# Layer 1's expert passes finished in their own turn, gathered outputs added earlier, and the late tiles' modulation written with dealt columns in its last step

## The chip, the cores and the metric

The kernel runs on one core of a Trainium2 chip. The metric is the device time of one execution in microseconds. A core has a matrix engine (PE, with its weight loads shown as PEld), a vector engine (DVE), a scalar engine (ACT), GpSimd (POOL), and SP, which here does little but issue transfers. "Q" behind an engine's name (SPq, ACTq) means its instruction queue: registers, branches, transfers. The core's transfers share 16 DMA engines.

## The reference, cut to what matters

Two layers of a transformer over 256 latent and 256 context rows of 1024 columns. Each layer ends in a mixture of experts:

```python
def modulate(x, shift, scale):
    return layer_norm(x) * (1 + scale) + shift

xl = layer_norm(ALPHA * xl + g1 * yl, ln1_g[l], ln1_b[l])       # after the output projection
yl = moe(modulate(xl, sh2, sc2), router_w, ...)                 # 16 experts, two of one group per row
xl = layer_norm(ALPHA * xl + g2 * yl, ln2_g[l], ln2_b[l])
```

An expert computes `(silu(h @ gate) * (h @ up)) @ down` with 256 hidden columns, so its weights are 1 MB each for gate, up and down. Layer 0 handles latent and context rows (four tiles of 128 rows), layer 1 only the latent rows (two tiles). The output is the latent rows after layer 1.

## The kernel before

**The rows before the experts.** `out_proj` (L1201) computes for each tile of 128 rows the residual and the first layer norm, then the rows that the experts read: `rows_modulate` (L1348, one DVE operation, (x - mean) * sc2) and, after the router has been worked out, `rows_shift` (L1353, one DVE operation, times r plus sh2). Both go over 128x1024 f32. The result, the tile hx, has its columns dealt: column p*8+t of x stands at t*128+p, because a later transpose takes blocks of 128 columns and the weights of an expert are loaded with p outside t. Before the change, modulate does the dealing: it reads x and sc2 at a step of 8 elements (`dealt`, L1344) and writes contiguously; shift reads hx contiguously and sh2 at a step of 8 elements, and writes hx in place. hx then goes to a table H in DRAM, from which POOL gathers the rows of a pass (xb), and for the first pass PE picks rows straight from hx (`block_pick`, xbp<-oh,hx).

In both layers the last two tiles' modulations sit at the end of `out_proj`: modulate of the tile before the last (p), then of the last one (end), the router's small DVE operations on "arena", then both shifts back to back, then the tables of the routing (ids of the experts in "metai", a flag "anyi" that rows overflowed, "oh" and "roh" for picking rows).

**The passes.** `moe` (L1911) works in passes of 128 rows; a pass covers one expert or several. Layer 0 has 11 passes, layer 1 has eight, over the units (0,1), (2,3), (4,7), (5,6), (8,11), (9,10), (12,15), (13,14); `end` is 7 there. A unit's expert is known only on the chip. The weights of units 0 to 3 (W0) are loaded before, at the end of `out_proj`. A pass is: rows transposed (xT), `gate_up` (32 matmuls of 512 columns for a pass of four segments, 16 for two; PE, pgu), `act` (ACT th, DVE ac twice, PE transposes acp, ACT acT), `down` (PE, y), and `rows_out` (copies yo, then one 0.5 MB write to the table Y, issued by ACT).

`fetch(p + 2)` in each turn (L1915) issues the weights of the pass two ahead from SP. `expert_steps` (L1772) splits one unit's load in three steps: half 0 of gate and up (2 x 0.5 MB, into a raw buffer, four of these), half 1 (2 x 0.5 MB, into a u buffer, eleven of these), and down (1 MB, u; every fifth load puts half 0 in u and down into two h buffers as two transfers of 0.5 MB). Two units of one pass were interleaved step by step:

```python
for fs in zip(*steps):
    for f in fs:
        f()
```

SP works its queue in order: a transfer whose buffer is not free holds all that stand behind it. A few hundred instructions for rows that overflow their pass stand behind a branch in each layer (`overflow`, L1848); it isn't taken in the profiled execution, but each engine passes through it at its place.

**The order of a turn.** The loop (L1957) does `gate_up(p)`, `rows_of(p + 1)`, `fetch(p + 2)`, and `finish(*prev)` (L1967), which is act, down and Y write of pass p-1. A scheduler then places these by priority, so that y(p-1) lands in the matmul stream inside gate_up(p+1). After the loop come the broadcast loads, the gathers of Y's rows (`y_gather`, L1900, per tile two indirect transfers from POOL of 0.5 MB each: yg), and the last two passes (L2073): down of pass end-1, kept on the core as ylast, gate_up of the last pass, its act and down. What ylast holds is added by matmuls (pcomb, in `part`); what was gathered is scaled and added to x by `scale` (L2015: ACT yg, then DVE yg) and `add` (L2020: DVE yg, DVE x). In layer 1 (`mod is None`) they stand around the ylast copies, tile 0's ahead of them and tile 1's behind. `join` (DVE rest, x), then norm and output end the kernel. In layer 0 the tail also loads and splits the next layer's first weights (`split`: wraw, whi, wlo).

Of the kernel before, what the change touches and what calls it, by code (L numbers as in the profile page):

```python
# [15 lines left out]
OP = mybir.AluOpType  # L16
# [4 lines left out]
P = 128  # L21
D = 1024
KT = D // P
# [129 lines left out]
class Net:  # L153
# [1190 lines left out]
    def dealt(x):  # L1344

        return x.rearrange("r (p t) -> r t p", t=KT)

    def rows_modulate(self, k):  # L1348
        self.hx.append(k.h)
        k.hd = k.h[:, :D].rearrange("r (t p) -> r t p", t=KT)  # L1350
        self.nc.vector.scalar_tensor_tensor(k.hd, self.dealt(k.x), k.mean, self.dealt(self.sc2[:, k.s, :]), op0=OP.subtract, op1=OP.mult)

    def rows_shift(self, k, eng=None):  # L1353
        self.nc.vector.scalar_tensor_tensor(k.hd, k.hd, k.r[1], self.dealt(self.sh2[:, k.s, :]), op0=OP.mult, op1=OP.add)
        (eng or self.nc.sync).dma_start(self.H[self.l][k.n * P:(k.n + 1) * P, :], k.h[:, :D])

    def rows_turn(self, k, between=None):
# [550 lines left out]
    def moe(self, l, xs, tiles, mod):  # L1908
        nc, T = self.nc, len(tiles)
        streams = (0, 1) if T == 4 else (0,)  # L1910
        plan = unit_passes(l)  # L1911
        end = len(plan) - 1
        W = self.W0

        def fetch(p):  # L1915
            steps = []
            for _, _, a in plan[p][1] if p <= end else []:
                if a not in W:
                    W[a], new = self.expert_steps(l, self.meta(a, 15, engines=[mybir.EngineType.SP]))
                    steps.append(new)  # L1920
            for fs in zip(*steps):
                for f in fs:
                    f()

# [2 lines left out]
        def gather(p):  # L1927
            if p <= end:
                xb[p] = self.route_index(plan[p][0])

        def rows_of(p):
            xT = self.h([P, KT, P], "xT")
            if p == 0:
                self.block_pick(self.first, xT, lambda: gather(1))
            else:
                self.block_turn(xb[p], xT)
            return xT

        def finish(p, ps):
            ys = [self.pw("y2"), self.pw("y3")] if (end - p) % 2 else [self.po("y0"), self.po("y1")]  # L1940
            self.down(plan[p][1], W, self.act(ps), ys)
            self.rows_out(ys, plan[p][0] * P, self.p([P, D], "yo"))

        blocks, prev, got = {0: rows_of(0)}, None, []
        if T == 4:
            self.overflow(l)
        fetch(0)
        fetch(1)
        for p, (_, segs) in enumerate(plan[:-1]):
            gather(p + 2)  # L1950
            if p == 0 and l < DEPTH - 1:
                self.announce(l + 1, "SP", self.last_idx)
            ps = self.gate_up(segs, W, blocks[p], self.pa("pgu"))
            if p == 0:
                self.early_mm = self.last_mm
                if T == 2:
                    self.overflow(l)  # L1957
                else:
                    with self.behind(self.last_idx, self.last_mm):
                        self.ada_end()  # L1960
                for n in range(0, T, 2):
                    self.route_gates(n)
                self.route_rest()
            blocks[p + 1] = rows_of(p + 1)
            fetch(p + 2)
            if prev:
                finish(*prev)  # L1967
            prev = p, ps
            if p == end - 2:
                self.pickT = self.h([P, T, 2, P], "pickT")  # L1970
                for n in range(T):
                    self.last_rows(n)
# [22 lines left out]
        def split():  # L1995
            if self.late:
                self.late.pop(0)()

        def part(n, a):
            g = bag[n]  # L2000
            if a == 0:
                g.ps = [al("pcomb") for al in (self.pa, self.pw)]
            for c in range(2):
                nc.tensor.matmul(g.ps[c], self.pickT[:, n, spot[a]], yl[:, a, c], start=a == 0, stop=a == 1 and mod is None)
# [10 lines left out]
        def scale(n):  # L2015

            nc.scalar.activation(got[n][0], got[n][0], AF.Copy, scale=self.gab[:, 0, n:n + 1])
            stt(got[n][0], got[n][1], self.gab[:, 1, n:n + 1], got[n][0], op0=OP.mult, op1=OP.add)  # L2018

        def add(n):  # L2020
            x, y, i = xs[tiles[n]], got[n][0], 0 if tiles[n] in LAT_TILES else 1
            nc.vector.tensor_mul(y, y, g2[:, i, :])  # L2022
            stt(x, x, ALPHA, y, op0=OP.mult, op1=OP.add)  # L2023
# [46 lines left out]
        if mod is None:  # L2070
            steps = (mul, -1), (join, 0), (shift, 1), (centre, 0), (root, 0)
        else:
            steps = ((unit, 2), (join, 0), (shift, 1), (turn, 2), (more, 0), (centre, 0), (root, 1), (root, 0), (low, 2), (mul, -1))  # L2073
        with self.ordered(last):
            self.down(plan[end - 1][1], W, self.act(psA), ysA)
            for c in range(2):
                nc.scalar.copy(yl[:, 0, c], ysA[c])
            acB = self.act_rows(self.gate_up(plan[end][1], W, blocks[end], self.pa("pgu")))
            part(0, 0)
            aT = self.act_turn(acB)  # L2080
            split()
            self.down(plan[end][1], W, aT, ysB)
            part(1, 0)
            if mod is None:
                scale(0)
                add(0)
            nc.vector.tensor_copy(yl[:, 1, 0], ysB[0])
            nc.scalar.copy(yl[:, 1, 1], ysB[1])
            if mod is None:
                scale(1)  # L2090
                add(1)
            split()
            for t in range(-1, T + 2):
                for f, k in steps:
                    if 0 <= t - k < T:
                        f(t - k, tiles[t - k])
# [130 lines left out]
```

## Time and profile before

| | |
|---|---|
| three runs | 992.14, 987.21, 992.06 us; median 992.06 us |
| the profiled execution | 991.99 us, of which 990.2 us lie between its first and last instruction |
| busy share of the span | PE 86%, DVE 56%, ACT 34%, POOL 18% |
| DMA, mean | 232 GB/s over the span; 230.04 MB |
| mean granted clock of TensorE | 0.948 of full speed |

The busy shares are means over stages with different limits, so they don't tell what a stage waits for. The stages here: attention and output projection of layer 0 up to about 400 us, its experts to about 570, the same for layer 1 up to about 830 and 990. In the rows further on, a time is us from the span's start, "x3" counts instructions, and in square brackets stands how long the engine was idle before, and what ended that. A DMA share of 1.0 means that all 16 DMA engines were busy.

### The profile page before, as it was taken

The page shows a single profiled execution, that of the slowest core. Times are in us where ns is not written, and L with a number is a line of the kernel's source. Part 1 is how long each engine was busy: PE and PEld are TensorE (multiplying, and loading weights), DVE is VectorE, ACT ScalarE, POOL GpSimd, SP SyncE. Part 2 cuts the span into 40 slices and gives each one's busy share as a digit, 9 for nine tenths or more (in the row PEclk, how much of TensorE's full clock was granted, in tenths as well). Part 3 has the DMA queues.
Part 4 walks back from the last instruction along what each step waited for, and adds up shares of the span by engine and source line. Part 5 has one row for each costly group of instructions (what it writes and reads, how often), then busy time and mean ns, then how long its engine had stood idle before and what let it go on. Part 6 is the DMA issues. An engine that isn't in the chain of part 4 may idle for free. (4 is left out here: it accounts for less than half of the span.)

```text
span 990.2 us, 12986 instructions
## 1 busy us (share of the span) xinstructions
PE 848.4 (86%) x4436; PEld 465.8 (47%) x4436; DVE 549.7 (56%) x1419; ACT 332.7 (34%) x783; POOL 175.1 (18%) x195
## 2 busy tenths in 40 slices
PE   4799999999898982999999798999978964997773
PEld 2476555545345860643333245756654653332221
DVE  4465777567666679622221287677777577221116
ACT  2243455534454220011112248455474420110111
POOL 1522110002250111100010225132253010000010
PEclk9989999999999995999999899999999995999987
DMA  9963756465553248899999862155422493999981
GB/s 329 316 225 96 255 161 229 141 221 192 216 170 110 88 155 313 313 376 333 379 399 387 320 191 93 55 194 152 159 92 100 143 348 122 362 398 411 391 316 42
DMA packets 82150, 230.04 MB, mean 232 GB/s; under 512 B 10144, under 2 KB 26112, under 8 KB 77984
## 3 DMA queue, kind: packets, MB, share of 16 engines
q1 hardware_dynamic: 66624, 184.74, 52.5%
q10 hardware_dynamic: 11280, 29.21, 8.1%
q0 software_dynamic: 4176, 15.21, 4.0%
q8 instruction: 37, 0.61, 0.2%
q14 instruction: 33, 0.27, 0.1%
HBM read 215.97 MB, written 16.84 MB: 235 GB/s over the span
## 5 line engine op out<-in xcount | busy, mean ns | idle before, releaser
L1802 PE MATMUL pgu<-egu,xT 128*32 128x512 f32 (+2 forms) x752 | 152.7, 606 | 10.3 <-DMA egu<-in_exp_w_up_dram 9.9
L1040 ACT ACTIVATE P<-S,nm 128x512 f32<-128x512 f32 (+1 forms) x120 | 73.3, 614 | 77.8 <-DVE nm L1029 56.4
L262 PE MATMUL pw<-whi,xhi 128*128 128x512 f32 (+1 forms) x224 | 94.1, 422 | 4.5 <-ACT xhi L474 3.6
L264 PE MATMUL pw<-whi,xlo 128*128 128x512 f32 (+1 forms) x224 | 90.2, 406 | 4.1 <-DVE xlo L525 3.4
L1814 DVE SCALAR_TENSOR_TENSOR ac<-th,pgu 128x256 f32<-128x256 f32 x19 | 8.0, 421 | 154.3 <-ACT th L1812 154.3
L1802 PEld LDWEIGHTS pgu<-egu,xT 128*32 128x32 f32 (+2 forms) x752 | 47.2, 128 | 95.2 <-issue 92.4
L263 PE MATMUL pw<-wlo,xhi 128*128 128x512 f32 (+1 forms) x224 | 90.7, 406 | 0.0
L1832 PE MATMUL y<-edn,acT 128*32 128x512 f32 (+2 forms) x376 | 77.5, 625 | 6.1 <-DMA edn<-in_exp_w_down_dram 5.0
L1029 DVE TENSOR_REDUCE nm<-S 128x1 f32<-128x512 f32 (+1 forms) x120 | 68.4, 595 | 15.5 <-PE S L1002 11.0
L262 PEld LDWEIGHTS pw<-whi,xhi 128*128 128x128 f32 x224 | 43.1, 193 | 31.8 <-issue 16.2
L363 PE MATMUL adaacc<-adaw,cst 128*32 128x512 f32 x256 | 54.1, 606 | 0.0
L1703 POOL DMA_INDIRECT xb<-H,ridx x17 | 16.4, 963 | 196.1 <-DVE ridx L1700 66.6
L1070 PE MATMUL PTp<-ident,P 128*128 128x128 f32 x320 | 46.6, 277 | 3.7 <-DVE P L1058 3.4
L252 POOL TENSOR_TENSOR wolo<-woraw,wohi 128x512 fp32r<-128x512 f32 x32 | 41.0, 1309 | 48.7 <-ACT wohi L251 48.7
L264 PEld LDWEIGHTS pw<-whi,xlo 128*128 128x128 f32 x224 | 43.0, 192 | 14.0 <-DVE xlo L525 4.7
L1812 ACT ACTIVATE th<-pgu 128x256 f32<-128x256 f32 x19 | 7.3, 385 | 122.1 <-PE pgu L1802 109.0
L1832 PEld LDWEIGHTS y<-edn,acT 128*32 128x32 f32 (+2 forms) x376 | 23.2, 130 | 53.1 <-issue 38.4
L1070 PEld LDWEIGHTS PTp<-ident,P 128*128 128x128 f32 x320 | 35.9, 140 | 25.0 <-issue 15.3
L263 PEld LDWEIGHTS pw<-wlo,xhi 128*128 128x128 f32 x224 | 43.0, 192 | 10.0 <-issue 1.3
L262 PE MATMUL pwo<-wohi,oT 128*128 128x512 f32 x96 | 38.9, 406 | 0.7 <-ACT oT L256 0.7
L1077 ACT COPY PT<-PTp 128x512 f32<-128x512 f32 (+1 forms) x60 | 30.9, 515 | 21.9 <-PE PTp L1070 18.4
L264 PE MATMUL pwo<-wohi,oT 128*128 128x512 f32 x96 | 38.0, 395 | 0.0
(407 smaller groups left out, 1551.9 us busy)
## 6 DMA issues: line engine op xcount, KB each, us to landing
adaw<-in_w_ada_dram SPq DMA_DIRECT2D x32, 1024.0 KB
egu<-in_exp_w_gate_dram SPq DMA_DIRECT2D x64, 512.0 KB
egu<-in_exp_w_up_dram SPq DMA_DIRECT2D x64, 512.0 KB
edn<-in_exp_w_down_dram SPq DMA_DIRECT2D x26, 1024.0 KB
adaw<-in_w_ada_dram SPq DMA_DIRECT2D x32, 512.0 KB
wraw<-in_w_in_dram SPq DMA_DIRECT2D x20, 512.0 KB
woraw<-in_w_out_dram SPq DMA_DIRECT2D x8, 1024.0 KB
Y<-yo ACTq DMA_DIRECT2D x15, 512.0 KB
```

The costliest lines, as they stand in the source:

```text
L252: eng.tensor_sub(lo[:, s], src[:, s], hi[:, s].bitcast(F32))
L262: mm(out, a[0], b[0], start=start, stop=False)
L263: mm(out, a[0], b[1], start=False, stop=False)
L264: return mm(out, a[1], b[0], start=False, stop=stop)
L363: self.nc.tensor.matmul(acc[32 * j:32 * j + 32, :], self.cst[:, k if row is None else row, :], t[:, j, :], start=(k == 0), stop=stop)
L1029: nc.vector.tensor_reduce(t.nm[:, j:j + 1], t.S[j][:, :t.nk], axis=AX.X, op=OP.max, negate=True)
L1040: self.last_exp = nc.scalar.activation(t.P[:, j, :t.nk], t.S[j][:, :t.nk], AF.Exp, bias=t.nm[:, j:j + 1], accum_out=t.l[:, j:j + 1])
L1070: nc.tensor.transpose(t.pt[n][:, k, :], t.P[:, n, k * P:(k + 1) * P], self.ident)
L1077: (nc.vector.tensor_copy if t.kind != "A" and n == 0 else nc.scalar.copy)(out, t.pt[n][:, 0:nkt, :])
L1703: self.last_fetch = nc.gpsimd.indirect_dma_start(out=xb, out_offset=None, in_=self.H[self.l][:, :], in_offset=bass.IndirectOffsetOnAxis(ap ...
L1802: self.last_mm = mm(ps[c:c + w, :].rearrange("r (c n) -> r c n", c=2), xT[:, kk, c:c + w], W[a][kk // 4][:, :, kk % 4, :], start=kk == 0, ...
L1832: mm(ys[n][c:c + w, :], aT[:, f, c:c + w], W[a][2][f][:, n * 512:(n + 1) * 512], start=f == 0, stop=f == 1)
```

## The change

It has four parts. In `fetch`, two units of a pass are loaded one after the other (half 0, half 1, down of the first, then of the second), in both layers; only the last pass keeps the interleaving. In layer 1, a pass up to end-2 is finished in its own turn of the loop, `finish(p, ps)`, not in the next one's. In layer 1's tail, scale and add of both tiles stand ahead of the last pass's act. For the late tiles (tiles 2 and 3 of layer 0, both of layer 1) modulate reads and writes contiguously, and shift reads contiguously and writes with dealt columns into another buffer "hd": neighbouring elements of its output lie 128 elements (512 bytes) apart.

```diff
--- before.py
+++ after.py
@@ -1345,13 +1345,27 @@
 
         return x.rearrange("r (p t) -> r t p", t=KT)
 
+    @staticmethod
+    def dealt_out(x):
+        return x[:, :D].rearrange("r (t p) -> r p t", t=KT)
+
     def rows_modulate(self, k):
+        k.late = k.n >= self.T - 2
+        out, x, sc = k.h[:, :D], k.x, self.sc2[:, k.s, :]
+        if not k.late:
+            out, x, sc = out.rearrange("r (t p) -> r t p", t=KT), self.dealt(x), self.dealt(sc)
+        self.nc.vector.scalar_tensor_tensor(out, x, k.mean, sc, op0=OP.subtract, op1=OP.mult)
+
+    def rows_shift(self, k, eng=None):
+        src, sh = k.h[:, :D], self.sh2[:, k.s, :]
+        if k.late:
+            k.h = self.h([P, D], "hd")
+            out, src, sh = self.dealt_out(k.h), src.rearrange("r (p t) -> r p t", t=KT), sh.rearrange("r (p t) -> r p t", t=KT)
+        else:
+            out = src = src.rearrange("r (t p) -> r t p", t=KT)
+            sh = self.dealt(sh)
+        self.nc.vector.scalar_tensor_tensor(out, src, k.r[1], sh, op0=OP.mult, op1=OP.add)
         self.hx.append(k.h)
-        k.hd = k.h[:, :D].rearrange("r (t p) -> r t p", t=KT)
-        self.nc.vector.scalar_tensor_tensor(k.hd, self.dealt(k.x), k.mean, self.dealt(self.sc2[:, k.s, :]), op0=OP.subtract, op1=OP.mult)
-
-    def rows_shift(self, k, eng=None):
-        self.nc.vector.scalar_tensor_tensor(k.hd, k.hd, k.r[1], self.dealt(self.sh2[:, k.s, :]), op0=OP.mult, op1=OP.add)
         (eng or self.nc.sync).dma_start(self.H[self.l][k.n * P:(k.n + 1) * P, :], k.h[:, :D])
 
     def rows_turn(self, k, between=None):
@@ -1918,7 +1932,7 @@
                 if a not in W:
                     W[a], new = self.expert_steps(l, self.meta(a, 15, engines=[mybir.EngineType.SP]))
                     steps.append(new)
-            for fs in zip(*steps):
+            for fs in zip(*steps) if p == end else steps:
                 for f in fs:
                     f()
 
@@ -1963,7 +1977,9 @@
                 self.route_rest()
             blocks[p + 1] = rows_of(p + 1)
             fetch(p + 2)
-            if prev:
+            if T == 2 and p < end - 1:
+                finish(p, ps)
+            elif prev and T == 4:
                 finish(*prev)
             prev = p, ps
             if p == end - 2:
@@ -2075,20 +2091,17 @@
             self.down(plan[end - 1][1], W, self.act(psA), ysA)
             for c in range(2):
                 nc.scalar.copy(yl[:, 0, c], ysA[c])
+            for n in range(T) if mod is None else ():
+                scale(n)
+                add(n)
             acB = self.act_rows(self.gate_up(plan[end][1], W, blocks[end], self.pa("pgu")))
             part(0, 0)
             aT = self.act_turn(acB)
             split()
             self.down(plan[end][1], W, aT, ysB)
             part(1, 0)
-            if mod is None:
-                scale(0)
-                add(0)
             nc.vector.tensor_copy(yl[:, 1, 0], ysB[0])
             nc.scalar.copy(yl[:, 1, 1], ysB[1])
-            if mod is None:
-                scale(1)
-                add(1)
             split()
             for t in range(-1, T + 2):
                 for f, k in steps:
```

SP, the weights of pass 2 in layer 1 (units 4 and 7; the first loads its down weights as two transfers). A register instruction ahead of each transfer is left out. Before:

```order
L1885 TENSOR_LOAD metai_7656
...
L1763 DMA egu_8525<-in_exp_w_gate_dram 128x1024
...
L1763 DMA egu_8525<-in_exp_w_up_dram 128x1024
L1885 TENSOR_LOAD metai_7656
...
L1763 DMA egu_8528<-in_exp_w_gate_dram 128x1024
...
L1763 DMA egu_8531<-in_exp_w_gate_dram 128x1024
...
L1763 DMA egu_8534<-in_exp_w_gate_dram 128x1024
...
L1763 DMA edn_8537<-in_exp_w_down_dram 128x1024
...
L1763 DMA edn_8541<-in_exp_w_down_dram 128x2x1024
```

And now:

```order
L1899 TENSOR_LOAD metai_7658
...
L1777 DMA egu_8529<-in_exp_w_gate_dram 128x1024
...
L1777 DMA egu_8529<-in_exp_w_up_dram 128x1024
...
L1777 DMA egu_8532<-in_exp_w_gate_dram 128x1024
...
L1777 DMA edn_8535<-in_exp_w_down_dram 128x1024
L1899 TENSOR_LOAD metai_7658
...
L1777 DMA egu_8539<-in_exp_w_gate_dram 128x1024
...
L1777 DMA egu_8542<-in_exp_w_gate_dram 128x1024
...
L1777 DMA edn_8545<-in_exp_w_down_dram 128x2x1024
```

Unit 4's second half and its down weights now stand ahead of unit 7's first half.

PE in layer 1, from pass 4's rows to the last pass, before (y_9023 is the down projection of pass 4, y_9118 of pass 5, y_9156 of pass 6):

```order
L1802 MATMUL pgu<-egu,xT 32x512
L1832 MATMUL y_9023<-edn,acT 32x512 x8
L1832 MATMUL y_9024<-edn,acT 32x512 x8
L1897 MATMUL lastp<-ident,lastoh 128x128 x2
L1802 MATMUL pgu<-egu,xT 32x512 x31
L1737 MATMUL xbp<-ident,xb 128x128 x8
L1822 MATMUL acp<-ident,ac 128x128 x4
L1832 MATMUL y_9118<-edn,acT 64x512 x4
L1832 MATMUL y_9119<-edn,acT 64x512 x4
L1832 MATMUL y_9156<-edn,acT 32x512 x8
```

And now (y_9059 is pass 5, y_9160 pass 6):

```order
L1816 MATMUL pgu<-egu,xT 32x512
L1836 MATMUL acp<-ident,ac 128x128 x2
L1911 MATMUL lastp<-ident,lastoh 128x128 x2
L1816 MATMUL pgu<-egu,xT 32x512 x2
L1846 MATMUL y_9059<-edn,acT 64x512 x4
L1846 MATMUL y_9060<-edn,acT 64x512 x4
L1911 MATMUL lastp<-ident,lastoh 128x128 x2
L1816 MATMUL pgu<-egu,xT 32x512 x29
L1751 MATMUL xbp<-ident,xb 128x128 x8
L1836 MATMUL acp<-ident,ac 128x128 x2
L1846 MATMUL y_9160<-edn,acT 32x512 x8
```

Inside gate_up(6) stood the down projection of pass 4; now it is that of pass 5, and so in each turn of layer 1.

DVE in layer 1's tail, before:

```order
L1814 SCALAR_TENSOR_TENSOR ac_9207<-th_9205,pgu_9188 128x256
L1815 SCALAR_TENSOR_TENSOR ac_9207<-ac_9207,pgu_9188 128x256
L2018 SCALAR_TENSOR_TENSOR yg_9147<-yg_9148,arena_7648,yg_9147 128x1024
L2022 TENSOR_TENSOR yg_9147<-yg_9147,bc_9142 128x1024
L2023 SCALAR_TENSOR_TENSOR x_7635<-x_7635,yg_9147 128x1024
L2087 COPY ylast_9155<-y0_9158 128x512
L2018 SCALAR_TENSOR_TENSOR yg_9151<-yg_9152,arena_7648,yg_9151 128x1024
L2022 TENSOR_TENSOR yg_9151<-yg_9151,bc_9142 128x1024
L2023 SCALAR_TENSOR_TENSOR x_7637<-x_7637,yg_9151 128x1024
```

And now:

```order
L2034 SCALAR_TENSOR_TENSOR yg_9151<-yg_9152,arena_7650,yg_9151 128x1024
L2038 TENSOR_TENSOR yg_9151<-yg_9151,bc_9146 128x1024
L2039 SCALAR_TENSOR_TENSOR x_7637<-x_7637,yg_9151 128x1024
L2034 SCALAR_TENSOR_TENSOR yg_9155<-yg_9156,arena_7650,yg_9155 128x1024
L2038 TENSOR_TENSOR yg_9155<-yg_9155,bc_9146 128x1024
L2039 SCALAR_TENSOR_TENSOR x_7639<-x_7639,yg_9155 128x1024
L1828 SCALAR_TENSOR_TENSOR ac_9219<-th_9217,pgu_9200 128x256
L1829 SCALAR_TENSOR_TENSOR ac_9219<-ac_9219,pgu_9200 128x256
L2103 COPY ylast_9159<-y0_9162 128x512
```

The six operations on yg and x stood behind the last pass's ac, three of them behind the ylast copy; now all six stand ahead of ac. ACT's two yg likewise stand ahead of the last pass's th, where they stood behind its acT.

## Rows read from the trace of the kernel before

**Rows 1.** Windows: us, PE PEld DVE ACT POOL busy (count), PEclk, DMA share, GB/s.

```profile
835.00:839.50 4.50, 4.37 (x24) 2.89 (x24) 1.51 (x13) 0.59 (x1) 0.66 (x1) 0.80 0.50 161
839.50:845.00 5.50, 5.48 (x25) 2.22 (x26) 2.74 (x14) 0.00 (x0) 0.28 (x1) 1.00 0.64 208
...
867.00:892.00 25.00, 23.14 (x156) 9.08 (x149) 6.84 (x20) 3.86 (x8) 1.88 (x2) 1.00 1.01 398
...
917.00:942.00 25.00, 19.50 (x135) 6.62 (x133) 4.20 (x8) 3.76 (x9) 0.00 (x0) 0.93 1.02 391
```

**Rows 2.** Timeline of SP in layer 1: start us, us, transfer issued.

```profile
831.64 0.34 SPq L1763 DMA_DIRECT2D egu<-in_exp_w_up_dram  x1
841.49 0.33 SPq L1763 DMA_DIRECT2D egu<-in_exp_w_gate_dram  x1
```

**Rows 3.** Waits of SP's queue, 780 to 990 us: us in all, times, longest.

```profile
SPq L1763 <- PE pgu L1802: 9.8, 2, 8.9
```

**Rows 4.** Timeline of PE, pass 0's gate_up in layer 1, behind the overflow branch.

```profile
839.52 6.19 PE L1802 MATMUL pgu<-egu,xT 128*64 128x512 f32 x26
```

**Rows 5.** The chain that ended last, its end: start us, us, what.

```profile
941.72 20.12 DMA edn<-in_exp_w_down_dram
...
961.88 5.93 PE y L1832 x14
...
968.43 1.06 ACT yg L2017
...
969.51 1.29 DVE yg L2018
...
970.83 1.23 DVE yg L2022
...
972.08 1.22 DVE x L2023
973.31 0.61 DVE rest L2032
```

**Rows 6.** Timeline of DVE at the end of layer 0's output projection.

```profile
370.32 2.09 DVE L1351 SCALAR_TENSOR_TENSOR hx<-x,lnm,bc 128x1024 f32<-128x1024 f32 x1
...
379.50 2.04 DVE L1351 SCALAR_TENSOR_TENSOR hx<-x,bmv,bc 128x1024 f32<-128x1024 f32 x1
```

**Rows 7.** Windows, layer 0; columns as in rows 1.

```profile
446.00:448.00 2.00, 2.00 (x24) 0.63 (x20) 0.00 (x0) 0.00 (x0) 0.00 (x0) 1.00 0.18 47
...
480.00:520.00 40.00, 38.11 (x198) 14.51 (x196) 10.00 (x29) 5.42 (x11) 5.29 (x5) 1.00 1.02 401
...
380.00:384.00 4.00, 0.00 (x0) 0.00 (x0) 3.38 (x13) 0.21 (x1) 1.96 (x1) 0.50 0.36 102
```

**Rows 8.** Timeline of ACT, layer 0's tail: the next layer's weights awaited.

```profile
565.45 1.90 ACT L555 CAST whi<-wraw 128x2048 fp32r<-128x2048 f32 x1 [5.01 <-DMA wraw<-in_w_in_dram]
```

**Rows 9.** Timeline of DVE at the end of layer 1's output projection.

```profile
808.44 1.28 DVE L1339 SCALAR_TENSOR_TENSOR hx<-x,bmv,bc 128x1024 f32<-128x1024 f32 x1
...
813.12 2.04 DVE L1351 SCALAR_TENSOR_TENSOR hx<-x,bmv,shsc 128x1024 f32<-128x1024 f32 x1
...
821.11 2.05 DVE L1354 SCALAR_TENSOR_TENSOR hx<-hx,lnr,shsc 128x1024 f32<-128x1024 f32 x1
```

**Rows 10.** Timeline of PE: layer 1's pcomb.

```profile
953.14 1.98 PE L2004 MATMUL pcomb<-ylast,pickT 128*128 128x512 f32 x4
...
967.73 5.42 PE L2004 MATMUL pcomb<-ylast,pickT 128*128 128x512 f32 x12
```

**Rows 11.** Timelines of ACT, POOL, DVE: last Y writes, first gather, first use.

```profile
929.14 0.33 ACTq L1837 DMA_DIRECT2D Y<-yo  x1
...
943.19 0.33 ACTq L1837 DMA_DIRECT2D Y<-yo  x1
...
952.00 0.94 POOL L1903 DMA_INDIRECT yg<-Y,yslot  x1 [47.51 <-DMA bc<-in_ln_g_dram]
...
962.58 1.28 DVE L2018 SCALAR_TENSOR_TENSOR yg<-yg,arena 128x1024 f32<-128x1024 f32 x1 [8.04 <-DMA yg<-Y,yslot]
```

## The prediction, made before the changed kernel was run

> **What bounds the kernel now.** I read the chain of waits first, backwards from the end, then windows with the DMA share along it, then the timelines of SP, DVE and PE at the places where that share falls.
>
> The chain ends so: a transfer of down weights of the last pass, issued at 941.72, lands 20.12 us later at 961.84; the last down projection takes 5.93 us; then ACT yg, three DVE operations on yg and x (1.06, 1.29, 1.23, 1.22 us), and at 973.31 the first rest, which opens the norm [rows 5]. So two things set the end of layer 1: when the stream of weights is through, and what stands between the last y and rest.
>
> The stream itself: from 867 to 892 and from 917 to 942 the DMA engines are full (share 1.01 and 1.02, 391 to 398 GB/s), with PE busy 23.14 and 19.50 of 25 us [rows 1]. There nothing helps but fewer bytes or an earlier start. The start is not full: from 835 to 839.5 the share is 0.50, to 845 it is 0.64 [rows 1]. That is 4.5*0.50 + 5.5*0.36 = 2.25 + 1.98 = 4.23 us of 16 idle engines. The reason stands in SP's timeline: after unit 4's first half (issued up to 831.64) the next transfer goes out at 841.49 [rows 2], and SP's longest wait for a gate-up matmul is 8.9 us [rows 3]. Unit 7's first half wants a raw buffer that pass 0 still reads, and all else stands behind it.
>
> Layer 0 looks alike on a smaller scale: its experts run with DMA share 1.02 from 480 to 520, PE busy 38.11 of 40 us, but 446 to 448 has 0.18 [rows 7], and at the end ACT waits 5.01 us for the next layer's weights until 565.45 [rows 8]. Those are the last transfers of the same stream.
>
> **The change part by part.** The sum is made against the profiled execution, 991.99 us; the median of the runs is 992.06, so the two may stand for each other.
>
> 1. *Modulate of late tiles, layer 0.* Two operations of 2.09 and 2.04 us read two operands at a step of 8 elements [rows 6]. With both contiguous they become what the same shape costs elsewhere with contiguous operands, 1.28 [rows 9]: 0.81 + 0.76 = 1.57 us. DVE is the path here: the second unit's weights are issued right behind the last modulate, and from 380 to 384 the DMA engines idle for 4*0.64 = 2.56 us [rows 7]. An earlier issue moves the saturated stream behind it, and with that the weights at 565.45. Taken in full: -1.57.
>
> 2. *Modulate, layer 1.* The last one, 2.04 us at 813.12 [rows 9], has the router behind it without a gap: -0.76. The one before it is followed by a wait for PE, so nothing.
>
> 3. *Shifts.* Each reads one operand at a step now and costs 2.05 [rows 9]; then it writes at a step of 128 elements and reads contiguously. No row shows such a write. Below it is bounded by 1.28, as if writes at a step were free; above there is no row, and I extend the bound under the rivals. I take 2.05: two operands at a step cost as much as one [rows 6, 9], so one stepped access in the operation seems to set its pace, whichever it is. Term 0, ends -0.77 each and open above. In layer 1 two of them lie on the path to the experts' ids; in layer 0 the stream of the second unit's weights, under way since the modulate, covers a small change.
>
> The Trainium skill, page "SBUF — State Buffer", section "Door 1: The DMA port swizzle", says that SBUF has lines of 16 bytes, that accesses staying in one run at full bandwidth, and that each access that crosses to a new line pays a penalty. It makes no difference between reads and writes, so by it a write at 512 bytes a step gains nothing over a read at 32; the sum by it stays what I have, and the case in which writes are free falls away.
>
> 4. *Weights unit by unit, layer 1.* Unit 4's second half (1 MB, a u buffer) no longer stands behind unit 7's first half: it waits only for the end of the shifts and goes out right behind 831.64. At the 395 GB/s of the full stream 1 MB is 2.65 us, so it fills the idle 2.25 us up to 839.5. Unit 4's down weights go into two h buffers and wait for PE to be past the overflow branch, which is where its gate-up goes on at 839.52 [rows 4]; they go out some 2 us before 841.49 and fill part of the 1.98 idle us up to 845, of which I count 0.75, an estimate: part of it was already taken by the transfers from 841.49 on. Together -3.0; ends: -1.5 (half of the hole, if the transfers share badly) and -4.23 (all of it). The stream behind is full, so this carries to 961.84.
>
> 5. *Weights unit by unit, layer 0.* The one clear hole, 2*0.82 = 1.64 us [rows 7], is of the same kind (SP held by a gate-up of the pass ahead, with free u buffers behind it). But PE is 95% busy behind it [rows 7], so an earlier stream partly turns into a wait for buffers. -1.0; ends 0 and -1.64.
>
> 6. *Finish in its own turn.* It saves nothing by itself: the same matmuls, and PE has 25 - 19.50 = 5.50 us idle in a late window [rows 1]. What it costs: y(p) now comes one to four gate-up matmuls after gate_up(p), so th, ac, acp and acT have less cover. That idle time hides it, except from 867 to 892, where only 1.86 us are free; see the first rival. What it moves: the last Y write takes the place of pass 4's, issued at 929.14 and not 943.19 [rows 11], 14.05 us earlier, and the gathers with it. They were issued 8.81 us behind that write, at 952.00, and first used at 962.58 [rows 11].
>
> 7. *Scale and add ahead of the last act.* After the last y there remain the ylast copies and pcomb. Four records of pcomb took 1.98 us [rows 10]. Four of the first twelve are free at 967.73, and rest needs two more: 6*0.495 = 3.0, so rest could start near 970.7 instead of 973.31. The four operations on the path last 4.80 us, of which 2.6 come back and PE holds the rest: -2.5; ends -1.5 (pcomb at a lower clock) and -4.8. What is queued behind the added work: th, ac and so the last y wait for the gathers. They come first used at 962.58 - 14.05 = 948.5; two times three DVE operations of 1.29 + 1.23 + 1.22 make 7.5 us, to 956.0; ac, acp and acT another 2 (an estimate), to 958.1. The down weights come at 961.84. Margin 3.7 us, both ends moving together with the stream.
>
> Sum: -1.57 - 0.76 - 0 - 3.0 - 1.0 - 0 - 2.5 = -8.8, so 991.99 - 8.8 = **983.2 us**.
>
> **The rivals.**
>
> *A, the filled holes don't carry.* The stream starts ahead but stalls again, because PE, with y(p) sooner and only 1.86 us free from 867 to 892, gives raw buffers back later; likewise in layer 0. For it: PE busy 23.14 of 25 and 38.11 of 40 us. Against it: the full DMA share of both late windows shows the stream and not PE as the limit. Terms 4 and 5 fall: 991.99 - 4.83 = 987.2.
>
> *B, stepped writes are free.* The two shifts of layer 1 fall to 1.28, 2*0.77 = 1.54 more: 981.7. Against it: no row shows a stepped operand for nothing.
>
> *C, the gathers come too late.* They share the engines with a full stream, and their buffers come free only after the rows of pass 6 and 7. If the first use is later than 948.5 + 3.7 = 952.2, each microsecond holds the last down projection by one. If moving the write brought them nothing, it would cost 14.05 - 3.7 = 10.35: 993.6, no change. Against it: the time from write to gather and from gather to use was taken under the same full stream.
>
> *D, stepped writes are dear (slower than before).* Place: the four shifts at the end of the two output projections. If one takes x us, layer 1 pays twice x - 2.05 on its path, and layer 0, once the second unit's weights are through, the same. The gains are gone at 4*(x - 2.05) = 8.8, x = 4.3; at three times the 2.05 it costs 16.4, and the kernel takes 999.6. For it: every element goes to another place, 512 bytes on, where rows have only 32. Against it: the stepped reads cost just 1.6 times the contiguous ones.
>
> **How the numbers follow.** Forecast 0.57, A 0.20, B 0.10, C 0.08, D 0.05. A measurement of this kernel tells about 0.5%, 5.0 us, from no change: faster is below 987.1. That holds the forecast, B and half of A: 0.77. Half of A and C are within: 0.18. D is slower: 0.05. The range: down to 983.2 less the far ends of terms 3, 4, 5 and part of 7, that is 1.5 + 1.2 + 0.6 + 2.3 = 5.6, so 977.5; up to A with 2.3 us of late gathers or of dearer shifts, so 989.5. C in full, D and a bit below are left out, under 0.2.
>
> **What would show it.** Right: modulates of 1.28 and shifts near 2.05; unit 4's second half issued near 832, DMA share from 835 to 850 near 0.9; the last down weights landing 6 us earlier than 961.84; gathers issued before 940; rest within 3 us of the last y. Wrong: shifts over 4 us; ACT or DVE waiting for yg with the last down weights landed; DMA share from 867 on falling below 0.95 with SP waiting for pgu.

## The result, and the profile after

Slower, by a little more than can be told from no change: 997.37 us median (994.04 to 1000.69) against 992.1 (987.21 to 996.83), ratio 1.0064 with a 95% interval of 1.0037 to 1.0091. Forecast were 983.2 us and a range to 989.5. The profiled execution has a span of 995.0 us, against 990.2 before.

The small parts came as forecast. DVE's timeline at the end of layer 1's output projection, after:

```profile
817.43 1.28 DVE L1357 SCALAR_TENSOR_TENSOR hx<-x,bmv,shsc 128x1024 f32<-128x1024 f32 x1
...
824.48 1.94 DVE L1367 SCALAR_TENSOR_TENSOR hd<-hx,lnr,shsc 128x1024 f32<-128x1024 f32 x1
```

Against [rows 9], modulate fell from 2.04 to 1.28, and the shift, now with its write at a step, from 2.05 to 1.94. From the last first-norm operation to the ids ("metai") layer 0 took 36.74 us before and 34.79 after, counted from the third tile's, and layer 1 16.96 and 15.84.

SP's timeline in layer 1, after, answers to [rows 2]:

```profile
834.83 0.34 SPq L1777 DMA_DIRECT2D egu<-in_exp_w_up_dram  x1
835.42 0.33 SPq L1777 DMA_DIRECT2D egu<-in_exp_w_gate_dram  x1
...
841.63 0.99 SPq L1777 DMA_DIRECT2D edn<-in_exp_w_down_dram  x2
```

Unit 4's second half goes out right behind its first, and the windows after (columns as in [rows 1]) have no hole behind the start:

```profile
839.00:850.00 11.00, 10.29 (x52) 4.29 (x50) 5.36 (x27) 1.56 (x3) 0.94 (x1) 1.00 0.99 374
850.00:940.00 90.00, 79.97 (x492) 26.48 (x490) 16.09 (x44) 10.60 (x22) 4.68 (x5) 0.96 1.01 391
```

So each edit did what it says, and time was lost elsewhere. Layer 0 shows the larger loss. ACT waits for the next layer's weights in two places; the second is the one of [rows 8]. Before (one line, the first place), then after (both places):

```profile
558.05 1.90 ACT L555 CAST whi<-wraw 128x2048 fp32r<-128x2048 f32 x1 [5.85 <-DMA wraw<-in_w_in_dram]
```

```profile
562.09 1.90 ACT L555 CAST whi<-wraw 128x2048 fp32r<-128x2048 f32 x1 [11.07 <-DMA wraw<-in_w_in_dram]
...
569.04 1.90 ACT L555 CAST whi<-wraw 128x2048 fp32r<-128x2048 f32 x1 [4.57 <-DMA wraw<-in_w_in_dram]
```

The last whi starts 173.77 us behind layer 0's ids (395.27), where it started 165.73 us behind them (from 399.72): 8 us more. In this stage the DMA engines idle more. The whole stage, before and after, and then the window after in which the share is lowest behind 420:

```profile
399.72:565.45 165.73, 153.23 (x849) 62.50 (x848) 45.90 (x131) 27.28 (x60) 18.86 (x20) 0.98 0.96 365
```

```profile
395.27:569.04 173.77, 155.15 (x849) 64.45 (x848) 45.93 (x131) 27.17 (x59) 18.85 (x20) 0.97 0.92 349
460.00:470.00 10.00, 9.50 (x68) 3.45 (x67) 3.56 (x8) 1.93 (x4) 0.94 (x1) 1.00 0.56 172
```

The shares of 0.96 and 0.92 make 6.6 and 13.9 us of 16 idle engines, so the added idle time is nearly the whole loss. From 460 to 470 the share was 1.01 and 391 GB/s before. SP's waits from 405 to 540, after, first three:

```profile
SPq L1777 <- PE y L1846: 19.4, 4, 12.4
SPq L1777 <- PE pgu L1816: 18.0, 5, 10.9
SPq L1777 <- DMA Y<-yo: 17.4, 3, 9.8
```

Before, the same stretch had 5.3 us of waits for y, 30.3 for pgu and 11.8 for Y writes. So SP waits longer for down projections and Y writes, and less for gate-ups.

The other loss is the tail. The chain of waits after, its end:

```profile
945.24 17.70 DMA yg<-Y,yslot
...
963.05 1.29 DVE yg L2034
...
964.37 1.24 DVE yg L2038
...
965.63 1.23 DVE x L2039
966.86 0.34 DVE ac L1828
...
968.85 6.35 PE y L1846 x16
975.20 2.79 PE pcomb L2020 x6
...
978.01 0.70 DVE rest L2048
```

What held the end before was a transfer of weights [rows 5]; now it is a gather, then scale and add, and only then the act of the last pass. In the tail itself the gain is there: 2.8 us from the last y to rest, where it was 5.5.

### The profile page after: what moved, and what is told of

It reads as the page before. It is cut to its first block, busy times and chain, and to the rows that moved or that the text cites. A ratio compares the mean times of both kernels' runs of the same rounds, so it can differ in the third digit from the quotient of the medians.

```text
span 995.0 us, 12998 instructions
## 1 busy us (share of the span) xinstructions
PE 849.4 (85%) x4436; PEld 463.0 (47%) x4436; DVE 545.1 (55%) x1419; ACT 332.7 (33%) x783; POOL 173.0 (17%) x195
## 5 line engine op out<-in xcount | busy, mean ns | idle before, releaser
L262 PE MATMUL pwo<-wohi,oT 128*128 128x512 f32 x96 | 39.0, 406 | 0.7 <-ACT oT L256 0.7
L212 POOL TENSOR_TENSOR lsr<-lsv,mhalf 128x1 f32<-128x1 f32 x18 | 14.6, 813 | 135.2 <-DVE lsv L210 132.0
```

What stands on the lines that cost most here:

```text
L262: mm(out, a[0], b[0], start=start, stop=False)
```

## The experiments

With each run go the ratio to the kernel before (with its 95% interval) and two stages of its one profiled execution, in us: from layer 0's ids to the start of the last whi, and from layer 1's ids to the end of the span. Kernels with the same layer 1 behind its ids differ by some us in the second stage (the kernel before 163.1, e4 165.1, e12 159.8), so it counts only where the ratio agrees. e8 has another output and no ratio, and is not in the table.

```
run                                            ratio   interval          layer 0  layer 1
changed kernel                                 1.0064  1.0037 to 1.0091  173.8    164.7
e1   layer 0 interleaved                       0.9997  0.9977 to 1.0017  167.2    165.8
e2   old places of scale and add               1.0004  0.9987 to 1.0021  173.5    161.3
e3   both                                      0.9953  0.9929 to 0.9977  166.7    162.4
e4   modulate and shift alone                  0.9953  0.9932 to 0.9974  167.7    165.1
e5   layer 0: downs last                       1.0045  1.0024 to 1.0066  170.6    166.5
e6   layer 0: own turn                         1.0114  1.0083 to 1.0145  175.2    164.9
e7   e3, scale and add behind the act          0.9938  0.9908 to 0.9967  166.9    160.4
e9   layer 0: raw halves first                 1.0005  0.9980 to 1.0030  165.5    165.0
e10  e3 without own turn                       0.9893  0.9855 to 0.9932  167.7    154.3
e11  e3 without unit by unit                   0.9951  0.9928 to 0.9973  167.0    161.4
e12  before, layer 0 unit by unit alone        1.0056  1.0032 to 1.0081  174.7    159.8
e13  e3, Y writes from POOL                    0.9906  0.9869 to 0.9943  167.4    155.4
e14  e3, broadcasts late                       0.9978  0.9952 to 1.0004  166.3    161.0
e15  e10, scale and add behind the act         0.9870  0.9832 to 0.9907  166.7    153.7
```

### Undoing the parts

**e1**, layer 0's loads interleaved again:

```diff
-            for fs in zip(*steps) if p == end else steps:
+            for fs in zip(*steps) if p == end or T == 4 else steps:
```

> The changed kernel, but layer 0 loads the units of a pass step by step again; layer 1 keeps the new order. Theory Q (queue): in layer 0 a unit's down weights now stand ahead of the next unit's first half, and SP waits for a down projection to free their buffer; that cost some 8 us between the routing and the next layer's first weights. Then this kernel comes out 5 to 8 us under the changed one (0.5 to 0.8%), 989 to 992 us, and SP's waits for y in layer 0 fall from 19 us to about 5. Rival N (noise): the place of those 8 us is chance of one execution; then it stays within 2 us of the changed kernel.

992.37 us, ratio 0.9997, 0.67% under the changed kernel: the order of layer 0's loads costs this, as theory Q said, and it isn't chance of one execution (N). SP's waits for y in layer 0 fell to 5.1 us.

**e2**, scale and add of layer 1 back around the ylast copies (the three lines ahead of `acB` taken out, the old ones put back).

> The changed kernel, but layer 1's scale and add stand again around the copies of the last outputs. Theory G (gathers): the operations ahead of the last act wait for gathers that take 15 to 18 us among the weights, and so hold the last down projection by about 6 us; with them back it starts with its weights, but the tail after it is 2.5 us longer again: 3 to 4 us under the changed kernel, 993 to 994.5 us. Rival S (stream): the last weights land late as well and set the end; then there is no gain, or a loss of 2.5 us.

993.4 us, ratio 1.0004, 0.60% under the changed kernel: theory G. In the profile the second stage is 3.4 us shorter, as forecast; by the ratio it is some 6 us, with an interval that takes in both. The chain ends with a transfer of down weights again.

**e3**, both.

> Both of the above at once: layer 0 interleaved, scale and add in their old places. By Q and G the two savings add: 985 to 988 us, faster than the kernel before by 4 to 7 us. By N and S it stays near 995 to 998.

988.29 us, 0.9953: the two savings of 0.67 and 0.60% give 1.1% together, so within the intervals they add.

**e4**, the kernel before with the new `rows_modulate` and `rows_shift` alone.

> The kernel before with the new modulate and shift of the late tiles alone. The trace of the changed kernel shows modulate at 1.28 us and shift at 1.94 to 2.02. Theory: this part is worth 1.6 us and more in layer 0 and 0.9 in layer 1, together 2.5 us, so a ratio near 0.9975. Rival: the earlier issue in layer 0 is swallowed by the wait of the stream's end, and only 0.9 us remain, not to be told from nothing.

987.73 us, 0.9953 (0.9932 to 0.9974). The operations save about 3.1 us by the traces above (1.95 + 1.12), and the interval (2.6 to 6.7 us) reaches to that; the rival, 0.9 us alone, lies outside it. e3 has the same ratio, so what is left of the change in e3, unit by unit in layer 1 and the own turn, brings nothing together that can be told.

**e12**, the kernel before with layer 0's unit-by-unit loads alone (`for fs in steps if p < end and T == 4 else zip(*steps)`).

> The kernel before with layer 0's unit-by-unit loads alone. If the costs add, as the first three experiments say, this is 0.6 to 0.7% slower than the kernel before, 997 to 998.5 us, and the time from layer 0's ids to the last whi grows from 165.7 to 172 us or more. If the loss needs the earlier modulate (the stream meeting PE earlier), it is under 0.3%.

997.8 us, 1.0056, and 174.7 us in layer 0: this part alone costs 0.56%, with the old modulate.

### Why the order costs in layer 0

**e5**, gate and up unit by unit, both down loads behind them:

```diff
+            if T == 4 and p < end:
+                steps = [[f for s in steps for f in s[:2]] + [s[2] for s in steps]]
```

> The changed kernel, but in layer 0 a pass's gate and up weights are still loaded unit by unit and both units' down weights behind them. Theory Q: what cost 7 us was the down load of the first unit, which wants a buffer that an earlier down projection still reads, standing ahead of the second unit's first half; then this kernel recovers most of it, 990 to 993 us, and the time from the ids of layer 0 to the last of the next layer's weights falls from 173.7 to some 167 us. Rival U (unit by unit as such: the second unit's halves come late, or half 1 of the first unit stands ahead): it stays at 996 to 998 us and 173 us.

995.66 us, 1.0045, and 170.6 us in layer 0. Neither: in the profile 3 us come back, in the ratio nothing clear of the intervals, and SP still waits 20.1 us for y. The down load ahead of the next unit is not all of it; it may be that the waits for y hold half 1 too, which e9 tests.

**e9**, both first halves, which go into raw buffers, then the rest unit by unit:

```diff
+            if T == 4 and p < end:
+                steps = [[s[0] for s in steps] + [f for s in steps for f in s[1:]]]
```

> The changed kernel, but in layer 0 both units' first halves (raw buffers) go out first, then half 1 and down of the first unit, then of the second. Downs last recovered 3.0 of 6.7 us in the trace and little of it in time, so Theory Q is widened to Q2: SP is held at any step that needs a u buffer, half 1 or down, since y of an earlier pass still reads it, and what interleaving gave was 2 MB into raw buffers ahead of that wait. By Q2 this kernel recovers 5 us and more: 989 to 993 us, ids to last whi in layer 0 near 167 to 169 us. Rival D2: a down load ahead of the second unit's half 1 costs as much by itself; then 994 to 997 us and 170 us or more.

992.52 us, 1.0005, and 165.5 us: all of it came back, as theory Q2 said. The window of e9 that was the hole, and its waits for y from 405 to 540:

```profile
460.00:470.00 10.00, 9.49 (x68) 3.45 (x66) 3.56 (x8) 1.93 (x4) 0.94 (x1) 1.00 0.98 365
```

```profile
SPq L1777 <- PE y L1846: 5.1, 1, 5.1
```

Half 1 and down share the u buffers, which a late down projection still reads; the raw buffers are freed by a gate-up. Interleaving put both units' raw halves, 2 MB, ahead of the step that waits. Unit by unit, the second one's raw half stood behind it; that it need not have waited there is what e9 shows.

**e6**, layer 0's passes finished in their own turn as well (`if p < end - 1: finish(p, ps)` for both layers).

> The changed kernel, with layer 0's passes finished in their own turn as layer 1's are. Theory Q says that the new order hurts layer 0 because its down projections come a turn late; with y(p) in its own turn the buffers come free a pass earlier, SP's waits for y in layer 0 (19.4 us) shrink below 8, and 4 to 7 us come back: 990 to 993 us. Rival P (PE has no slack in layer 0, busy 38 of 40 us): the shorter cover of the act costs as much as it brings, 996 to 1000 us.

1003.1 us, 1.0114, so slower still, beyond what Q and P had, though the waits for y did shrink, to 9.4 us. SP's waits from 405 to 540:

```profile
SPq L1777 <- DMA Y<-yo: 30.5, 3, 10.8
SPq L1777 <- PE pgu L1816: 22.9, 5, 11.6
SPq L1777 <- PE y L1846: 9.4, 3, 5.8
```

A new wait took the place of the old one, three times some 10 us for Y writes. Whether it was these or PE's shorter cover (rival P) was not told apart in layer 0; layer 1 has the same waits, and there e13 tells.

### Why the gathers were late

**e8**, e1's kernel without the loads of layer 1's last pass: its two units use weights that are on the core already, so the output is another one.

> The first experiment's kernel without the loads of layer 1's last pass: its two units use the weights of a unit of the pass before, so 6 MB less are loaded (the output is another one). Theory G, sharing: the gathers took 12.6 to 18.3 us because the last pass's weights were under way; without these they land in 5 to 10 us. Rival I: they are slow where they now stand for another reason (right behind the last Y write); then they still take over 12 us.

How long the four gathers took from issue to landing, after, then in e1, then in e8:

```profile
DMA to landing us min/median/max: 11.3/15.2/17.7
```

```profile
DMA to landing us min/median/max: 12.6/16.0/18.3
```

```profile
DMA to landing us min/median/max: 7.6/7.7/7.7
```

Sharing: 7.7 us without the last pass's weights, which in the changed kernel are issued among them (the gathers from 941.51 to 945.24, the last three down loads at 942.80). Before, 8.7 to 9.3: at 952 the last weights had been issued for 10 us.

**e7**, e3 with scale and add of both tiles behind the last act, ahead of the ylast copies, and both of these on ACT.

> Layer 0 interleaved as in the first experiment; scale and add of both tiles behind the last act and ahead of the last outputs' copies, which both go to ACT. Nothing that the last down projection needs waits for a gather, and nothing but pcomb is left between it and rest. Theory G: 1 to 2.5 us under the kernel with the old places (988.3 us), 986 to 987. Rival: the gathers land so late that DVE's six operations end behind pcomb, and it equals 988.

985.47 us, 0.9938 (0.9908 to 0.9967), 0.15% under e3 and within its interval: nothing waits for a gather that shouldn't, but no gain over the old places can be told.

### What the own turn does in layer 1

**e10**, e3 with layer 1's finish a turn later again (`if prev: finish(*prev)`).

> The kernel of the third experiment (layer 0 interleaved, old places of scale and add) without the finish in its own turn: so modulate and layer 1's unit-by-unit loads alone. SP's waits for Y writes in layer 1 (28 to 30 us) fall back to some 8. If finishing early costs through these waits (theory L), it is 1 to 3 us faster than the third (988.3 us); if the full stream hides them, it is within 1.5 us of it.

980.74 us, 0.9893: 0.6% under e3, more than either theory had. So unit by unit in layer 1 is worth 0.6% over e4, and the own turn takes it back. Both differences are only just clear of the intervals (0.15 to 1.0%); the times at which SP is through with its loads, under e13, say the same.

**e11**, e3 with all loads interleaved: modulate and own turn alone.

> The kernel of the third experiment without any unit-by-unit loads: modulate and finish in its own turn alone. If the filled hole at the start of layer 1 is worth 3 us as forecast (theory F), this is 2 to 4 us slower than the third kernel, 990 to 992 us, and the time from layer 1's ids to the end grows from 162.4 to 164 or more. If the stream evens it out, it stays at 988 to 989.

987.08 us, 0.9951, the same as e3 and e4: the own turn by itself costs nothing that can be told, and the loads bring nothing beside it. The two work on one another. SP's longest waits from 835 to 960 in e3, then in e10, then the one line on Y in e11:

```profile
SPq L1777 <- DMA Y<-yo: 30.5, 3, 10.6
```

```profile
SPq L1777 <- DMA egu<-in_exp_w_gate_dram: 16.3, 14, 4.1
SPq L1777 <- DMA Y<-yo: 14.1, 2, 8.0
```

```profile
SPq L1777 <- DMA Y<-yo: 17.0, 3, 6.2
```

The changed kernel has 28.0 us in three such waits. Its chain of waits shows what hangs on one:

```profile
883.50 7.48 DMA Y<-yo
890.98 0.02 issue
890.99 0.33 SPq L1777
...
892.26 8.53 DMA edn<-in_exp_w_down_dram
900.79 0.02 issue
900.81 12.11 DMA egu<-in_exp_w_up_dram
...
913.06 1.98 PE pgu L1816 x4
```

SP stands still until a Y write lands, then issues, and a gate-up waits for that until 913.06.

**e13**, e3 with layer 1's Y writes issued by POOL:

```diff
-        self.last_out = self.nc.scalar.dma_start(self.Y[row:row + P, :], yo[:, :D])
+        self.last_out = (self.nc.gpsimd if self.T == 2 else self.nc.scalar).dma_start(self.Y[row:row + P, :], yo[:, :D])
```

> The third experiment's kernel (own turn, layer 1 unit by unit) with layer 1's Y writes issued by POOL instead of ACT. The tenth, without the own turn, is 0.6% faster than the third. Theory L (shared queue of transfers): SP's weight loads wait for Y writes that were issued before them in the program but start only after their pass (30.5 us in the third, 14.1 in the tenth); writes from POOL go through another queue, so these waits vanish, and the kernel comes within 2 us of the tenth: 980 to 984 us. Rival A (ACT and PE order: the earlier act has too little cover, or the broadcast loads hold ACT): the waits vanish and the time stays at 986 to 989. POOL's row gathers then stand behind the writes, which may take some of the gain.

982.03 us, 0.9906 (0.9869 to 0.9943), and no wait of SP for a Y write is left in layer 1: theory L. That is 0.5% under e3, only just clear of the intervals. SP's last weights, in the kernel before, in e3, e10 and e13:

```profile
938.59 3.52 SPq L1763 DMA_DIRECT2D edn<-in_exp_w_down_dram  x3
```

```profile
938.06 2.57 SPq L1777 DMA_DIRECT2D edn<-in_exp_w_down_dram  x3
```

```profile
930.24 1.92 SPq L1777 DMA_DIRECT2D edn<-in_exp_w_down_dram  x3
```

```profile
928.67 4.16 SPq L1777 DMA_DIRECT2D edn<-in_exp_w_down_dram  x3
```

Counted from layer 1's ids (827.12, 823.10, 822.95 and 824.78), SP is through after 115.0 us before, 117.5 in e3, 109.2 in e10 and 108.1 in e13; e11 has 114.9, the changed kernel 114.8. So unit by unit brings SP some 6 us forward, the own turn takes that back, and with the writes on POOL it comes again: the own turn then costs nothing beside the unit-by-unit loads. The move also takes six issues off ACT, which no run separates from it. What ties SP's load to ACT's write isn't shown either: it is no buffer, since yo comes from another pool (p) than the weights (raw, u, h).

**e14**, e3 with the three broadcast loads behind the ylast copies.

> The third experiment's kernel with layer 1's three broadcast loads of the tail issued by ACT behind the copies of ylast instead of ahead of the act of the last pass but one. In the third's chain ACT waits there until 943 us with acT, and PE's y(6) with it. Theory A: this wait is what the own turn costs; then 2 to 6 us come back, 982 to 986 us. Theory L: SP's waits for Y writes stay at 30 us and the last weights come as late; within 1.5 us of the third (988).

988.34 us, 0.9978 (0.9952 to 1.0004): no gain, and SP still waits 27.8 us for Y writes. Theory A falls. e13, measured beside it, is 0.7% faster.

**e15**, e10 with scale and add as in e7.

> The tenth experiment's kernel with scale and add of both tiles behind the last act and ahead of the last outputs' copies, both on ACT. In the tenth the gathers come at 952, after the last down projection, so six DVE operations and not the weights set the end: nothing is left to gain but the copy of 0.7 us that stood between them on DVE; 979.5 to 981 us, the same as the tenth within what can be told.

977.81 us, 0.9870 (0.9832 to 0.9907): with e10 the fastest, not to be told from it, and 1.3% faster than the kernel before. PE and the gathers at its end:

```profile
948.96 4.27 PE L1846 MATMUL y<-edn,acT 128*64 128x512 f32 x16 [0.46 <-ACT acT L1838]
```

```profile
953.78 1.28 DVE L2032 SCALAR_TENSOR_TENSOR yg<-yg,arena 128x1024 f32<-128x1024 f32 x1 [6.07 <-DMA yg<-Y,yslot]
```

The last y waits only for its act, and is through before the first gather is used: the weights no longer set the end.

## Why the prediction was wrong, point by point

*Steps 1 to 3, modulate and shift.* Right for the operations: 1.27 to 1.28 us and 1.94 to 2.02 us; rivals B and D did not come. By the Trainium skill, page "SBUF — State Buffer", section "Door 1: The DMA port swizzle", each access that crosses to a new line pays; the trace agrees for writes, 1.94 us against 1.28, and a write at a step of 512 bytes was no dearer than a read at 32. Forecast were 2.3 us, e4 measured 4.4 (0.47%, interval 0.26 to 0.68%), of which the traces explain 3.1; the rest is within the interval. Where it was gained is not shown. Nine kernels with the new modulate and layer 0's loads interleaved took 166.3 to 167.7 us from layer 0's ids to the last whi, the kernel before 165.7 in its one profile, so a part of layer 0's gain ahead of the ids may have been lost again by the end of its stream; "taken in full" stays open.

*Step 4, unit by unit in layer 1.* The mechanism was right and its size too small: without the own turn it is worth 0.6%, some 6 us (e10 against e4, with an interval of 1.6 to 10), where I took 3.0 and bounded it at 4.23. (The lower end that I gave, 1.5, is half of the term; half of the hole would have been 2.1.) SP is through with its loads 5.8 us sooner than before. I counted only the idle time of the engines at the start. e10 gains at the end too:

```profile
947.49 3.71 PE L1846 MATMUL y<-edn,acT 128*64 128x512 f32 x16 [0.46 <-ACT acT L1838]
```

All 16 matmuls of its last down projection run in 3.71 us, with no wait for weights. Before, PE waited 5.01 us for the last weights, and the 14 matmuls behind that wait took 5.93 [rows 5]. The granted clock from 940 to 952 is 1.00 in e10 (2.4 GHz); before, with PE busy 5.12 of the 10 us from 957 to 967, it was 0.66 there, a mean of 2.4 and 1.2 GHz.

*Step 5, unit by unit in layer 0.* This step failed first: "-1.0; ends 0 and -1.64", and it was +5.5 (e12) and +6.6 us (e1). I took the hole at 446, saw that SP was held there by a gate-up with free u buffers behind, and did not ask what the new order would be held by. In layer 0 the down projection comes a turn late, so a u buffer is the one that comes free last, and the new order puts two steps that want one ahead of the second unit's raw half (e5, e9). Rival A had the sign nearly (no gain), by another mechanism: PE as the bound, giving raw buffers back late.

*Step 6, the own turn.* "It saves nothing by itself" held (e11), "That idle time hides it" did not. I looked at PE's cover for the act, and the loss came through SP's queue: I moved the Y writes a turn earlier in the program and did not follow which transfers then stand behind them. It took back all of step 4 (e3, e10), and by e13 it did so through SP's waits for Y writes. In the changed kernel SP is through with its loads 114.8 us behind the ids, as before (115.0), so the last weights were not issued sooner, let alone landed the 6 us earlier that I had named as a sign.

*Step 7, scale and add.* The saving was right (rest 2.8 us behind the last y), and the margin was wrong: "the time from write to gather and from gather to use was taken under the same full stream" is the sentence that failed. The last Y write was issued at 933.78 and the gathers from 941.51. Layer 1's ids came 3.2 us later than before; counted from them, that is 1.5 and 0.4 us behind the forecast. But the gathers took up to 17.7 us in place of 9.3, and the first was used on DVE 15.2 us behind its issue and not 10.58. The second tile's had to be waited for again: the six operations on DVE took from 956.7 to 966.86, 10.2 us and not 7.5. Rival C happened, with a chance of 0.08: 3.4 us in the profile and some 6 by the ratio (e2).

So of the terms -1.57, -0.76, -3.0, -1.0 and -2.5, the first two came in sum (e4), the third was taken back by a term of 0, and the last two changed sign.

## What to carry to other kernels

Before a queue's order is changed, work out for each of its steps which buffer it wants, and who frees that last: put the steps whose buffers come free early ahead of the one that will wait. When a write is moved earlier in the program, look at every transfer of other engines that is queued behind it, since a program-order place and a place in time are two things. A transfer's duration belongs to the traffic around it: a gather's time at the end of a stream is no price for a gather ahead of the last burst.

## What the runs showed that I had not expected

A weight load issued by SP waits for a Y write issued by ACT, up to 10.8 us at a time (e6), and not for one issued by POOL (e13), though the two share no buffer.

The same four gathers took 6.7 to 6.8 us (e15, issued from 945.7 on, behind the last weights), 8.7 to 9.3 (before) and up to 17.7 (after).

A shift that writes at a step of 128 elements and reads contiguously takes 1.94 to 2.02 us; one that reads at a step of 8 and writes contiguously 2.05 to 2.13.
